# Storing eight bias rows once and repeating them from DRAM to DRAM, in place of eight stores that each repeat one partition's row

## The chip, the cores and the metric

The kernel runs on one core of a Trainium2 chip. A core has a matrix engine (PE, with its weight loads shown apart as PEld), a vector engine (DVE), a scalar engine (ACT), a general engine (POOL) and a sequencer that issues transfers (SP). Here all transfers are issued by SP, and 16 DMA engines carry them out. The metric is the time of one launch on the device in microseconds (us), lower is better. The median of three runs of the kernel before is 2368.28 us (2366.44 to 2369.18).

## The reference, cut to what matters

The program is two transformer blocks one after the other, on 1024 tokens of width 1024, in float32. The first block has a sparse attention branch (each query attends to 256 keys that an index score picks), a recurrent branch, a convolution branch, three gates and an MLP; the second block has latent attention and a pooling branch. The change touches the bias of the first block's attention. Each of the 8 heads adds a bias that depends only on the distance between query and key:

```
bias = rel_bias[_t5_bucket(t[None, :, None] - idx)]      # 32 buckets, 8 heads
logits = jnp.where(valid, logits + bias, -inf)
```

Beyond some distance the bucket is always the last one, so the bias is constant there; a constant added to all logits of a row drops out of the softmax. Only the near part, two blocks of 128 keys, has to be added, as a difference to that constant.

## The kernel before, in words

**The near bias.** Lines 667 to 681 make one row of 384 numbers for each head: a small matmul (line 672) of the bias table with a one-hot matrix gives an 8 x 384 result, from which DVE takes the far value away (line 676), into the tile `tr`: head h lies in partition h, 1536 bytes long. In the attention a tile of 128 queries by 256 keys needs this row shifted by one element for each query, that is, a different start in each partition. The kernel gets the shift from DRAM: the array `nbt` holds, for each head, the row of 384 numbers 128 times one after the other (192 KB for a head), and it is read back with a row length of 383 instead of 384 (line 681), so that each partition starts one element later. Lines 678 to 680 write `nbt`: eight transfers, one for each head, each of which reads the one partition of that head 128 times.

**Who reads it.** `unit_a` (line 730) is the first half of an attention unit for a pair of heads j and a block b of queries. At b = 7, the first block of each pair, it loads the near bias of the two heads from `nbt` into `nb_t`, a part of the constant tile `CP` (line 733, "CP<-nbt" in the trace); POOL adds it to the mask (line 743).

**What else SP issues there.** The weights come in pieces of 512 KB through `load_raw` (line 143; line 146 in the trace, "wr<-w_in", "wr<-w_up_conv") into two buffers `wr`. Each piece is split by `split_w` (line 194) into a high part H (ACT, which shows as line 138, "ws<-wr") and a rest L (POOL, line 199) in two buffers `ws`; a `wr` buffer is free again when POOL is done with it. PE multiplies from `ws` (`fm`, line 212, matmul at line 223): for each of the k tiles H times the high part of the data, H times its rest, and L times its high part. In the stretch where the near bias is written the program is in the loop of lines 625 to 633: a gate (a weight piece, 48 matmuls, a tanh on ACT, "th") and a mix with the convolution branch ("mx", stored by SP at line 632, "mix<-mx"), in turn. Between them run the steps of `search` (lines 495 to 588), which finds each query's 256th largest score bit by bit: DVE counts at line 535, ACT counts at line 538 ("jd<-sc,thrA"), and small DVE steps at lines 540 to 545.

**What sets the order.** The text of the kernel gives the data flow; the framework orders the instructions of each engine from it (the option `schedule_with_timeline_sim` in line 32) and adds the waits. Each engine, SP too, then runs its instructions in that fixed order: an instruction that waits holds up all that stand behind it on its engine. In the trace this order differs from the text: the rows of the near bias, which stand behind the loop of lines 625 to 633 in the text, are issued inside it, and the first two loads of `CP` from `nbt` stand between the fourth and the fifth of the eight stores.

Of the kernel before, what the change touches and what calls it, by code (L numbers as in the profile page):

```python
# [77 lines left out]
def tile_net(ctx: ExitStack, tc, a, out):  # L78
    nc = tc.nc
    PE, ACT, DVE, POOL, SP = nc.tensor, nc.scalar, nc.vector, nc.gpsimd, nc.sync  # L80
# [22 lines left out]
    def page(dt=F32, s="pg"):  # L103
        shape = [128, 4096 if dt == I8 else 2048 if dt == BF16 else 1024]
        if s in TEMPS:
            return tpp.tile(shape, dt, tag="tp", name=nm(s))
        return pgp.tile(shape, dt, tag="pg", name=nm(s))
# [12 lines left out]
    def stage(s="st", dt=F32):  # L120
        return stp.tile([128, 1024], dt, tag="st", name=nm(s))
# [7 lines left out]
    def dram(shape, s):  # L129
        return drp.tile(shape, F32, tag=s, name=s)  # L130
# [261 lines left out]
    for i in range(NB):  # L392
        j = page(s="junk")
# [13 lines left out]
    for j in range(2):  # L407
        for ps, cs in fm(next(wgen), hT):
            for e in range(2):
                S = SA[2 * j + e]  # L410
                o = 64 * e
# [263 lines left out]
    tr = stage("tr")  # L675
    DVE.tensor_scalar(out=tr[0:8, 0:384], in0=ps[0:8, 0:384], scalar1=far[0:8], scalar2=None, op0=ALU.subtract)
    nbt = dram([8, 128 * 384], "nbt")
    for h in range(8):
        SP.dma_start(out=nbt[h:h + 1].rearrange("o (p j) -> o p j", j=384),  # L679
                     in_=tr[h:h + 1, 0:384].unsqueeze(1).to_broadcast([1, 128, 384]))  # L680
        nbd.append(nbt[h, 127:127 + 383 * 128].rearrange("(p j) -> p j", j=383)[:, 0:256])

    VS, KK, QQ = [], {}, {}
# [839 lines left out]
    for pr_ in range(2):  # L1523
# [6 lines left out]
        for e in range(2):  # L1530
            o = 64 * e
# [203 lines left out]
```

## Time and profile before

| what | value |
| --- | --- |
| median of three runs | 2368.28 us (2366.44 to 2369.18) |
| the profiled execution's own time | 2365.88 us |
| its span, first to last instruction | 2364.0 us |
| PE busy | 2254.2 us, 95% of the span |
| DVE, ACT, POOL busy | 1442.4, 910.2 and 814.6 us |
| mean granted PE clock | 0.979 of full speed |
| all transfers | 228.89 MB on SP's queue, 31.8% of the 16 DMA engines' time |

The profile was taken of one execution; 1.88 us of its time lie outside its span. A busy share is an average over the whole span; what holds a stretch up is read from the waits and from the order of events inside that stretch. An issue on SP is short unless something keeps it: the time of an issue row is the time that SP spent on the instruction, not that of the transfer.

### The profile page before, as it was taken

To read this page: it belongs to the slowest core of one execution; us is meant where nothing else is said; L and a number is where in the kernel's file an instruction comes from. 1 tells how busy PE (TensorE), PEld (TensorE's weight loads), DVE (VectorE), ACT (ScalarE), POOL (GpSimd) and SP (SyncE) were. 2 spreads that over 40 slices of the span, in tenths; PEclk is the share of its full clock that TensorE was granted. 3 is DMA by queue.
4 is the path that set the end of the run, shared out by engine and by line. 5 is a ranking of instruction groups with operands and counts; after the bars stand their busy time and mean duration, and the time that the engine had idled before them with its cause. 6 is when DMAs were issued, how large, how long until landed. Compare 5 with 4: busy or idle time off the path is not lost.

```text
span 2364.0 us, 29829 instructions
## 1 busy us (share of the span) xinstructions
PE 2254.2 (95%) x11311; PEld 1899.9 (80%) x11311; DVE 1442.4 (61%) x2559; ACT 910.2 (39%) x1459; POOL 814.6 (34%) x524
## 2 busy tenths in 40 slices
PE   8999499999999999989999999998999999888998
PEld 6888387888888888878878888886888888677898
DVE  3589466354444377975576767595432768755655
ACT  5346241454445343523443333331111444345640
POOL 3221123344443222356245646322222236431036
PEclk9999799999999999999999999999999999899999
DMA  3113822212211211254233342652321254342341
GB/s 125 45 38 57 71 74 66 72 54 62 71 61 50 78 36 36 90 200 148 98 96 112 102 125 89 218 204 90 125 80 54 76 152 143 116 153 95 97 174 73
DMA packets 219076, 230.87 MB, mean 98 GB/s; under 512 B 12507, under 2 KB 189358, under 8 KB 218926
## 3 DMA queue, kind: packets, MB, share of 16 engines
q1 hardware_dynamic: 218926, 228.89, 31.8%
q8 instruction: 91, 1.49, 0.3%
q14 instruction: 59, 0.48, 0.1%
HBM read 166.47 MB, written 61.08 MB: 96 GB/s over the span
## 4 chain that ended last, share of the span: by engine, by line
PE 73%; DVE 12%; DMA 4%; issue 4%; POOL 3%; SPq 2%; ACT 2%; POOLq 0%; DVEq 0%; ACTq 0%
PE fm L223 43%; PE fm L354 15%; PE sp L1682 3%; PE sp L1566 2%; PE sp L262 1%; DVE jd L535 1%; PE sp L754 1%; PE py L790 1%; PE sp L910 1%; SPq L679 1%; PE sp L783 1%; DMA wr<-w_in 1%; DMA wr<-w_mlp_up 1%; POOL wf L329 1%; PE py L1608 1%
## 5 line engine op out<-in xcount | busy, mean ns | idle before, releaser
L223 PE MATMUL fm<-hH,ws 128*128 128x512 f32 (+1 forms) x1952 | 625.0, 395 | 32.3 <-ACT ws L138 31.8
L199 POOL TENSOR_TENSOR ws<-wr,ws 128x1024 fp32r<-128x1024 f32 (+2 forms) x123 | 288.7, 2347 | 851.9 <-ACT ws L138 805.6
L354 PE MATMUL fm<-xf,wf 128*128 128x512 f32 x2100 | 485.3, 392 | 1.6 <-POOL wf L329 0.9
L354 PEld LDWEIGHTS fm<-xf,wf 128*128 128x128 f32 x2100 | 395.6, 189 | 85.4 <-POOL wf L329 2.5
L223 PEld LDWEIGHTS fm<-hH,ws 128*128 128x128 f32 (+1 forms) x1952 | 366.2, 188 | 109.7 <-ACT ws L138 32.2
L223 PE MATMUL fm<-hL,ws 128*128 128x512 f32 (+1 forms) x976 | 386.1, 396 | 0.0
L223 PE MATMUL fm<-uH,ws 128*128 128x512 f32 x1024 | 319.6, 392 | 0.9 <-DVE x L1269 0.9
L138 ACT ACTIVATE ws<-wr 128x1024 fp32r<-128x1024 f32 (+2 forms) x124 | 126.0, 1016 | 417.4 <-PE fm L223 219.1
L223 PEld LDWEIGHTS fm<-uH,ws 128*128 128x128 f32 x1024 | 193.2, 189 | 41.9 <-DVE x L1269 1.1
L223 PEld LDWEIGHTS fm<-hL,ws 128*128 128x128 f32 (+1 forms) x976 | 184.0, 189 | 36.3
L329 POOL TENSOR_TENSOR wf<-sf,wf 128x512 fp32r<-128x512 f32 x100 | 152.8, 1537 | 150.5 <-ACT wf L138 141.7
L223 PE MATMUL fm<-uL,ws 128*128 128x512 f32 x512 | 199.9, 391 | 0.0
L362 DVE TENSOR_TENSOR kp<-kp,fm 128x512 f32<-128x512 f32 x167 | 113.9, 683 | 117.9 <-PE fm L354 111.6
L1269 DVE TENSOR_TENSOR x<-x,fm 128x512 f32<-128x512 f32 x128 | 87.0, 683 | 159.3 <-PE fm L223 152.8
L329 POOL TENSOR_TENSOR wf<-wr,wf 128x512 fp32r<-128x512 f32 x75 | 114.6, 1534 | 97.7 <-ACT wf L138 94.4
L138 ACT ACTIVATE p<-p,sml 128x896 f32<-128x896 f32 (+7 forms) x128 | 97.0, 773 | 65.1 <-DVE sml L760 41.3
L223 PE MATMUL fm<-spH,ws 128*128 128x512 f32 x352 | 116.5, 397 | 0.0
L223 PEld LDWEIGHTS fm<-uL,ws 128*128 128x128 f32 x512 | 96.6, 189 | 19.7
L189 DVE TENSOR_TENSOR PT<-sp,PT 128x512 fp32r<-128x512 f32 (+2 forms) x136 | 75.8, 576 | 59.6 <-ACT PT L138 58.4
L535 DVE TENSOR_SCALAR_CACHE_REDUCE jd<-sc,thrD 128x384 int8<-128x384 f32 (+1 forms) x124 | 100.6, 812 | 2.9
L138 ACT ACTIVATE jd<-sc,thrA 128x896 int8<-128x896 f32 (+1 forms) x62 | 67.8, 1094 | 48.2 <-DVE thrA L545 47.4
L138 ACT ACTIVATE PT<-sp 128x512 fp32r<-128x512 f32 (+2 forms) x136 | 64.7, 505 | 55.9 <-PE py L790 26.6
(395 smaller groups left out, 3882.5 us busy)
## 6 DMA issues: line engine op xcount, KB each, us to landing
wr<-w_in SPq DMA_DIRECT2D x78, 512.0 KB
wr<-w_mlp_up SPq DMA_DIRECT2D x32, 512.0 KB
ud<-t SPq DMA_DIRECT2D x32, 512.0 KB
wr<-w_mlp_down SPq DMA_DIRECT2D x32, 512.0 KB
uL<-ud SPq DMA_DIRECT2D x32, 512.0 KB
gate<-th SPq DMA_DIRECT2D x16, 512.0 KB
th<-gate SPq DMA_DIRECT2D x16, 512.0 KB
wr<-w_out SPq DMA_DIRECT2D x16, 512.0 KB
```

The costliest lines, as they stand in the source:

```text
L138: return ACT.activation(out=out, in_=in_, func=func, **kw)
L189: DVE.tensor_tensor(out=L, in0=src, in1=f(H), op=ALU.subtract)
L199: POOL.tensor_tensor(out=L, in0=v, in1=f(H), op=ALU.subtract)
L223: PE.matmul(ps[0:M], w_[:, k, :], x_[:, cs], start=(k == 0 and i == 0), stop=(k == kt - 1 and i == 2))
L262: PE.transpose(out=ps[:, (i - n0) * 128:(i - n0 + 1) * 128], in_=t, identity=ident[0:t.shape[0], 0:t.shape[0]])
L329: POOL.tensor_tensor(out=L, in0=src, in1=f(H), op=ALU.subtract)
L354: ins = PE.matmul(ps, w_[:, j, :], x_, start=(j == 0 and i == 0), stop=(j == J - 1 and i == 2))
L362: DVE.tensor_tensor(out=dst, in0=add, in1=ps, op=ALU.add)
L535: DVE.tensor_scalar(out=jd[:, 0:W], in0=sc[b][:, 0:W], scalar1=th[:, i:i + 1], scalar2=None, op0=ALU.is_ge, op1=ALU.add, accum_out=cnt[gna ...
L1269: DVE.tensor_tensor(out=x1[m][:, cs], in0=x1[m][:, cs], in1=ps, op=ALU.add)
L1566: PE.matmul(ps[:, 0:e - o], l_[:, qs], r_[:, cs], start=(n == 0), stop=(n == 4))
L1682: PE.matmul(po, l_[:, ts], r_, start=(k == 0 and n == 0), stop=(k == 7 and n == 2))
```

## The change

The eight stores of the loop become two transfers. The first stores the 8 x 384 tile once, one row from each partition, into a new DRAM array `nbr` (12 KB). The second, which depends on the first, reads each of the eight rows of `nbr` 128 times and writes all of `nbt` (1.5 MB). What `nbt` holds, its readers and all else stay.

```
     nbt = dram([8, 128 * 384], "nbt")
+    nbr = dram([8, 384], "nbr")
+    SP.dma_start(out=nbr, in_=tr[0:8, 0:384])
+    SP.dma_start(out=nbt.rearrange("h (p j) -> h p j", j=384), in_=nbr.unsqueeze(1).to_broadcast([8, 128, 384]))
     for h in range(8):
-        SP.dma_start(out=nbt[h:h + 1].rearrange("o (p j) -> o p j", j=384),
-                     in_=tr[h:h + 1, 0:384].unsqueeze(1).to_broadcast([1, 128, 384]))
         nbd.append(nbt[h, 127:127 + 383 * 128].rearrange("(p j) -> p j", j=383)[:, 0:256])
```

## Rows read from the trace of the kernel before

**Rows 1.** The page, part 2: the span in 40 equal slices of 59.1 us.
```profile
PE   8999499999999999989999999998999999888998
...
PEclk9999799999999999999999999999999999899999
```

**Rows 2.** Waits, 220 to 292 us: total us, times, longest us.
```profile
ACT ws L138 <- DMA wr<-w_in: 34.0, 1, 34.0
...
PE fm L223 <- ACT ws L138: 31.8, 1, 31.8
```

**Rows 3.** Timeline of PE, 252 to 292 us: start us, us, what.
```profile
251.75 0.39 PE L223 MATMUL fm<-spL,ws 128*128 128x512 f32 x1
...
254.01 0.39 PE L223 MATMUL fm<-spH,ws 128*128 128x512 f32 x1
286.23 0.79 PE L223 MATMUL fm<-hH,ws 128*128 128x512 f32 x1 [31.82 <-ACT ws L138]
...
290.75 0.40 PE L223 MATMUL fm<-hL,ws 128*128 128x512 f32 x1
```

**Rows 4.** Timeline of SP, 180 to 300 us: start us, us, issues.
```profile
187.01 0.37 SPq L146 DMA_DIRECT2D wr<-w_up_conv  x1
...
224.80 13.12 SPq L679 DMA_DIRECT2D nbt<-tr  x4
237.96 14.39 SPq L733 DMA_DIRECT2D CP<-nbt  x2
252.40 13.62 SPq L679 DMA_DIRECT2D nbt<-tr  x4
266.13 7.11 SPq L146 DMA_DIRECT2D wr<-w_in  x1
...
280.73 0.38 SPq L146 DMA_DIRECT2D wr<-w_in  x1
```

**Rows 5.** Stretches: us, busy of each engine, granted clock, DMA share, GB/s.
```profile
225.00:226.00 1.00, 1.00 (x6) 0.84 (x5) 0.96 (x3) 1.00 (x2) 0.00 (x0) 1.00 0.98 385
...
240.00:244.00 4.00, 4.00 (x19) 3.34 (x18) 3.93 (x7) 1.54 (x3) 2.38 (x1) 1.00 0.84 26
...
260.00:266.00 6.00, 0.00 (x0) 0.00 (x0) 0.00 (x0) 0.00 (x0) 0.00 (x0) 0.50 0.87 27
...
283.00:284.00 1.00, 0.00 (x0) 0.00 (x0) 0.00 (x0) 0.00 (x0) 0.00 (x0) 0.50 1.10 361
```

**Rows 6.** Chain that ended last, 215 to 345 us: start us, us, what.
```profile
224.24 0.53 DVE tr L676
...
266.13 18.90 DMA wr<-w_in
```

**Rows 7.** Timeline of POOL, 185 to 330 us.
```profile
235.34 2.40 POOL L199 TENSOR_TENSOR ws<-wr,ws 128x1024 fp32r<-128x1024 f32 x1 [13.14 <-ACT ws L138]
...
286.25 2.37 POOL L199 TENSOR_TENSOR ws<-wr,ws 128x1024 fp32r<-128x1024 f32 x1 [42.24 <-ACT ws L138]
```

**Rows 8.** Timeline of ACT, 232 to 292 us.
```profile
250.59 0.58 ACT L138 ACTIVATE th<-fm 128x512 f32<-128x512 f32 x1
285.12 1.06 ACT L138 ACTIVATE ws<-wr 128x1024 fp32r<-128x1024 f32 x1 [33.95 <-DMA wr<-w_in]
```

**Rows 9.** Stretches around one weight load (columns as in rows 5).
```profile
188.00:189.00 1.00, 1.00 (x6) 0.84 (x5) 0.96 (x3) 0.97 (x3) 0.00 (x0) 1.00 0.81 170
189.00:190.00 1.00, 1.00 (x6) 0.81 (x5) 1.00 (x3) 0.83 (x2) 0.00 (x0) 1.00 1.00 352
190.00:191.00 1.00, 1.00 (x6) 0.84 (x5) 1.00 (x2) 0.00 (x0) 0.00 (x0) 1.00 0.01 2
```

**Rows 10.** Stretch while `ln_g_2` (line 1644) is read 128 times (columns as rows 5).
```profile
2244.00:2244.50 0.50, 0.50 (x6) 0.50 (x6) 0.50 (x1) 0.50 (x2) 0.00 (x0) 1.00 0.90 352
```

**Rows 11.** Stretch behind the stall (columns as in rows 5).
```profile
340.00:350.00 10.00, 10.00 (x46) 8.28 (x45) 0.00 (x0) 1.84 (x3) 1.41 (x1) 1.00 0.32 100
```

**Rows 12.** Waits on transfers elsewhere, whole span: total us, times, longest us.
```profile
ACT wf L138 <- DMA wr<-w_mlp_up: 57.2, 8, 9.0
```

## The prediction, made before the changed kernel was run

> **What bounds the kernel now.** I read the page's slices first. PE is busy in nine tenths of nearly every slice; the one that stands out is the fifth (236 to 295 us), with PE at 4 tenths and a granted clock of 7 tenths [rows 1]. The waits of that stretch say why: PE waits 31.8 us, once, for the split of a weight piece on ACT, and ACT waits 34.0 us, once, for a transfer of `w_in` [rows 2]. PE's own timeline puts the hole between 254.0 and 286.2 us [rows 3]. All engines stand still in it [rows 5], since each has work in its fixed order that needs PE or ACT.
>
> The timeline of SP shows what kept the transfer [rows 4]. The eight stores of `nbt` begin at 224.80, as soon as DVE has written `tr` [rows 6]. The eight stores and the two loads of `CP` among them take SP 41 us to issue (13.12 + 14.39 + 13.62): the queue behind them is full, so each issue waits for room. The `w_in` piece that PE will miss is issued only at 266.13 and is used by ACT 18.9 us later [rows 4, 6]. Its buffer had been free since 237.74, when POOL ended the split before last (235.34 + 2.40) [rows 7]. So SP's order and its full queue delay it, nothing else.
>
> Why the queue is full is in the stretches: while the stores run, the DMA engines are busy 0.84 to 0.87 of the time and move only 26 to 27 GB/s [rows 5]. Around it, storing a full 128-partition tile goes at 385 GB/s and loading a weight piece at 361 [rows 5]. Eight stores of 196,608 bytes at 27 GB/s are 58 us. What sets them apart is their source, one partition read 128 times.
>
> **The change part by part.**
>
> *Removed: eight stores, 58 us of transfer and about 27 us of SP.* The gain is not these 58 us but what PE loses by them. PE's first matmul behind the hole begins at 286.23; without it, it would follow the one at 254.01 by the usual step. That step is 0.226 us: between 251.75 and 254.01 ten matmuls begin one after the other [rows 3]. So it would begin at 254.24: 31.99 us earlier. [...] That is 2.49 us more [rows 3]. Together 34.5 us.
>
> *Added: one store of 12 KB and a wait.* SP issues it at 224.8, waits until it has landed, and issues the repeat. An unqueued weight load shows such a round trip: issued at 187.01, moving in 188 to 190, nothing left after 190 [rows 4, 9]; 3.0 us in all, of which 512 KB (524,288 bytes) at 361 GB/s take 1.45, so some 1.6 us are fixed. I give the small store the whole 3.0, since a tile's store stands ahead of it. The repeat is issued at 227.8. Nothing behind SP's wait is due: the next weight buffer is free at 237.74 only [rows 7]. Cost nothing.
>
> *Added: the repeat, 1,572,864 bytes from DRAM to DRAM.* No row shows a transfer with both ends in DRAM. From one side, each end alone: 361 to 385 GB/s [rows 5], and reading one DRAM row 128 times is no hindrance by itself (`ln_g_2` for 128 partitions: 352 GB/s) [rows 10]. That gives 4.4 us. From the other side, the 27 GB/s of the stores if the destination were to blame: 58 us. I take 8.7 us, half the load's rate, because both ends load the same memory; it is nearest to the rows with a DRAM end. With 1.6 us fixed it lands at 227.8 + 1.6 + 8.7 = 238.1.
>
> *Moved: the wait of the `CP` loads.* Before, each needed its head's store; now both need the whole repeat, and SP stands still until then if they keep their place ahead of the `w_in` piece. Behind them are that piece and the mix store. Two issues of 0.4 us put the piece at 238.9; the CP loads' 262 KB take 0.7 us of its way, so it lands at 238.9 + 0.7 + 3.0 = 242.6.
>
> When is it due? Not before 251.2: ACT's order has the tanh of 250.59 (0.58 us) ahead of that split [rows 8]. So 8.6 us are to spare, and the repeat may take up to 17.3 us (91 GB/s) before anyone waits for it. From there each further us costs one. ACT's split then ends at 252.2 and POOL's, 2.4 us [rows 7], at 254.7; PE can begin at 254.24 with the two matmuls that need H alone and wants L at 254.69. What is left of the hole is 0.1 us, or 0.2 to be careful.
>
> *What is late next.* DVE's and ACT's work in the hole's place moves with PE. Behind it DVE has room: it stands idle from 340 to 350 while PE is full [rows 11], so PE sets the pace and carries the gain on. All later work waits for work, not for a time of day; I find nothing that gives it back.
>
> [...] The trace shows all sixteen engines at work on the old stores, 0.84 to 0.87 busy [rows 5]. [...]
>
> The sum: 34.5 - 0.2 = 34.3 us. The profiled execution took 2365.88 us (a span of 2364.0 and 1.88 outside), so it would take 2331.6. It was 2.4 us under the median of 2368.28; on the median the forecast is 2334.0.
>
> **The rivals.**
>
> *The repeat is slow, and part of the hole stays.* For it: no row shows such a transfer, and few engines or one memory at both ends could bring it below 91 GB/s. Against it: every row with a DRAM end is at over three times that. At 60 GB/s it takes 26 us, 9 past the limit; the half clock comes back too (2.5), so the gain is 34.3 - 11.5 = 22.8: 2345.5. At 42 GB/s (37 us) it is 2356.5.
>
> *Slower: the destination is what is slow, and the `CP` loads wait for all of it.* Before, SP went on behind the stores of two heads; now it stands until all eight are written. With 58 us the repeat lands at 227.8 + 1.6 + 58 = 287.4, the piece at 287.4 + 0.8 + 0.7 + 3.0 = 291.9, and ACT begins its split 6.8 us later than at 285.12 [rows 8]: 2375. It decides from 51 us on (31 GB/s). Were the repeat to run on a single engine, a sixteenth of 361 GB/s, it would take 70 us: 2387. Against it: the mix store writes DRAM at 385 GB/s [rows 5].
>
> *The order changes elsewhere.* The framework orders the whole program from its own reckoning, in which eight transfers become two. SP's order already differs from the text [rows 4], so a piece may now come sooner or later somewhere. The nearest price is what late weight pieces cost elsewhere: eight waits of 57.2 us in all on ACT, 9.0 the longest [rows 12]. I take two average ones of 7.2, 15 us, to either side of the forecast: 2319 to 2349. For it speaks only that nothing fixes the order; against it, that the changed transfers hang together with nothing but the `CP` loads, whose reader comes only in the attention, behind the whole search.
>
> **How the numbers follow.** The forecast, hole gone and order as before: 0.60. A slow repeat: 0.15. Slower: 0.08. Another order: 0.17. The likeliest gives 2334. The range goes from 2322 to 2356: it leaves out the slower case (0.08), a repeat beyond 37 us (some 0.03) and the ends of another order (some 0.04). About 0.2% (4.7 us) is what a measurement of this kernel can tell from no change. Faster by more than that: 0.60, 0.13 of the slow repeat and 0.15 of the other orders, 0.88; within it 0.04; slower 0.08.
>
> **What would show it.** Right, if PE's hole between 254 and 286 is gone, the fifth slice has PE and clock at 9, SP issues the `w_in` piece by 247 in place of 266.13, ACT's wait of 34.0 us for it is gone, and DVE still has its idle stretch before the end of the search. The repeat's duration shows as the stretch of high DMA share behind 228 us: 8.7 us by my value. Wrong, if that stretch is longer than 17 us and ACT still waits for the piece; or if the hole is gone and PE's idle time turns up elsewhere, in another order of its work. If DMA engines stay busy at 27 GB/s, the partition was not to blame and the main step falls.

## The result, and the profile after

The changed kernel takes 2332.26 us (median of 4 runs, 2330.53 to 2334.7) against 2368.28 (2366.44 to 2369.18): a ratio of 0.985, 95% interval 0.9833 to 0.9867. The forecast was 2334.0, in 2322 to 2356, with 0.88 on faster. The profiled execution took 2330.53 us, its span is 2328.3 us.

The page of the changed kernel, part 2 (40 slices of 58.2 us), against [rows 1]: the fifth slice is as full as the others, with the clock at full (1.00 in the stretches from 220 to 290 us).

```profile
PE   8999999999999999899999999989999999889998
...
PEclk9999999999999999999999999999999999899999
```

PE's timeline there, against [rows 3] (start us, us, what): the matmul that came 31.99 us late now follows the last one of the mix by one usual step.

```profile
253.74 0.39 PE L223 MATMUL fm<-spH,ws 128*128 128x512 f32 x1
253.97 0.39 PE L223 MATMUL fm<-hH,ws 128*128 128x512 f32 x1
254.20 0.39 PE L223 MATMUL fm<-hL,ws 128*128 128x512 f32 x1
```

SP's timeline, against [rows 4]. Two issues stand in place of eight, none of these issues takes longer than 0.81 us, and the `w_in` piece goes out at 238.29 in place of 266.13.

```profile
224.54 0.29 SPq L679 DMA_DIRECT2D nbr<-tr  x1
226.86 0.80 SPq L680 DMA_DIRECT2D nbt<-nbr  x1
237.37 0.81 SPq L734 DMA_DIRECT2D CP<-nbt  x2
238.29 0.38 SPq L146 DMA_DIRECT2D wr<-w_in  x1
```

SP's own waits, 200 to 292 us (total us, times, longest): the two that the change brought.

```profile
SPq L734 <- DMA nbt<-nbr: 9.7, 1, 9.7
...
SPq L680 <- DMA nbr<-tr: 2.0, 1, 2.0
```

Stretches of the changed kernel (columns as in [rows 5]; the last two are DMA share and GB/s): the repeat moves from 228.4 to 237.0 us, at 194 to 206 GB/s in the full microseconds between, half of the engines busy (share 0.52 to 0.54). DVE still has its idle stretch before the end of the search, from 300 to 316 us here.

```profile
228.00:229.00 1.00, 1.00 (x6) 0.84 (x5) 0.96 (x9) 0.40 (x2) 0.00 (x0) 1.00 0.30 88
...
230.00:231.00 1.00, 1.00 (x6) 0.84 (x5) 0.96 (x3) 1.00 (x2) 0.00 (x0) 1.00 0.53 198
...
300.00:316.00 16.00, 16.00 (x72) 13.28 (x71) 3.66 (x8) 3.21 (x4) 4.79 (x3) 1.00 0.32 99
```

ACT and POOL split the piece when their order reaches it, against [rows 7, 8]; neither waits for a transfer. POOL's first row is the split that frees the buffer for the piece.

```profile
250.81 1.05 ACT L138 ACTIVATE ws<-wr 128x1024 fp32r<-128x1024 f32 x1
```

```profile
235.10 2.40 POOL L199 TENSOR_TENSOR ws<-wr,ws 128x1024 fp32r<-128x1024 f32 x1 [13.15 <-ACT ws L138]
...
251.94 2.40 POOL L199 TENSOR_TENSOR ws<-wr,ws 128x1024 fp32r<-128x1024 f32 x1 [8.17 <-ACT ws L138]
```

PE's 11311 matmuls stand in the same order in both traces, so the same matmul can be compared by its place. The 1080th begins 0.27 us earlier in the changed kernel, the 1120th 34.75 us, the last 36.24. The hole and the slow clock behind it are 34.75 - 0.27 = 34.48 us of that. The other 1.8 us come before 224 us (0.27) and, mostly, near 650 us, far from any changed instruction; in two kernels below with the same median time, e1 and e3, the lead over the kernel before is 0.14 and 1.04 us at the 1080th, 34.62 and 35.52 at the 1120th, which is 34.48 in both again, and 33.0 and 35.2 at the end. I take what lies outside the hole for the spread between executions.

### The profile page after: what moved, and what is told of

Same layout as the page of the kernel before. It is cut to its first block, busy times and chain, and to the rows that moved or that the text cites. A ratio compares the mean times of both kernels' runs of the same rounds, so it can differ in the third digit from the quotient of the medians.

```text
span 2328.3 us, 29820 instructions
## 1 busy us (share of the span) xinstructions
PE 2249.2 (97%) x11311; PEld 1896.3 (81%) x11311; DVE 1441.3 (62%) x2559; ACT 910.1 (39%) x1459; POOL 813.2 (35%) x524
## 4 chain that ended last, share of the span: by engine, by line
PE 81%; DVE 9%; issue 3%; POOL 2%; DMA 2%; ACT 2%; SPq 0%; DVEq 0%; POOLq 0%; ACTq 0%
PE fm L223 49%; PE fm L354 16%; PE sp L1683 3%; PE sp L1567 2%; PE sp L262 1%; PE sp L755 1%; PE py L791 1%; PE sp L911 1%; PE sp L784 1%; DMA wr<-w_mlp_up 1%; PE py L1609 1%; POOL wf L329 1%; DVE mt L1136 0%; DVE PT L189 0%; DVE bc L271 0%
## 5 line engine op out<-in xcount | busy, mean ns | idle before, releaser
L329 POOL TENSOR_TENSOR wf<-sf,wf 128x512 fp32r<-128x512 f32 x100 | 152.7, 1536 | 151.8 <-ACT wf L138 141.6
L189 DVE TENSOR_TENSOR PT<-sp,PT 128x512 fp32r<-128x512 f32 (+2 forms) x136 | 75.8, 576 | 59.2 <-ACT PT L138 58.2
```

The source lines that it names most:

```text
L189: DVE.tensor_tensor(out=L, in0=src, in1=f(H), op=ALU.subtract)
L329: POOL.tensor_tensor(out=L, in0=src, in1=f(H), op=ALU.subtract)
```

## The experiments

Theory: sixteen engines that all read one SBUF partition move 27 GB/s; the queue behind these stores delays one weight piece past the moment when PE needs it; the piece has some 8 us to spare, and each us beyond costs one. The rivals are the number of transfers, the writing of DRAM, and SP's waits. "Above" is the median less 2332.3. The kernel before, run again beside each set of these, had medians of 2367.0 to 2367.4 us, about 1 us under the 2368.28 above; the ratios go by these.

| run | edit | median us (range) | ratio to before [95%] | above |
| --- | --- | --- | --- | --- |
| e1 | eight repeats, from DRAM | 2332.02 (2330.86 to 2333.32) | 0.9848 [0.9831, 0.9864] | -0.3 |
| e6 | one transfer, one partition | 2372.24 (2370.74 to 2374.28) | 1.0019 [1.0008, 1.0029] | 39.9 |
| e2 | one transfer, eight partitions | 2344.74 (2343.92 to 2346.59) | 0.9904 [0.9887, 0.992] | 12.4 |
| e9 | partitions 0 and 1 | 2379.47 (2375.55 to 2380.6) | 1.0049 [1.0026, 1.0072] | 47.2 |
| e10 | partitions 0 and 4 | 2347.72 (2343.71 to 2350.86) | 0.9917 [0.9888, 0.9946] | 15.4 |
| e3 | copies outermost | 2332.3 (2330.93 to 2335.12) | 0.9855 [0.9838, 0.9871] | 0.0 |
| e4 | chain of two repeats | 2338.02 (2335.07 to 2341.4) | 0.9874 [0.9858, 0.9891] | 5.7 |
| e7 | chain of three repeats | 2347.4 (2345.64 to 2351.34) | 0.9913 [0.9896, 0.9929] | 15.1 |
| e5 | four repeats, no wait | 2346.41 (2344.14 to 2348.48) | 0.991 [0.9893, 0.9926] | 14.1 |
| e8 | old stores, spread out | 2333.92 (2330.68 to 2335.02) | 0.9854 [0.9837, 0.987] | 1.6 |

### The source or the number: e1 and e6

e1 keeps the row store and makes eight transfers of the repeat again:

```
-    SP.dma_start(out=nbt.rearrange("h (p j) -> h p j", j=384), in_=nbr.unsqueeze(1).to_broadcast([8, 128, 384]))
+    for h in range(8):
+        SP.dma_start(out=nbt[h:h + 1].rearrange("o (p j) -> o p j", j=384),
+                     in_=nbr[h:h + 1].unsqueeze(1).to_broadcast([1, 128, 384]))
```

> The row store to DRAM stays, but the repeat is again eight transfers, one for each head, now read from DRAM. Theory (the source, one SBUF partition read by all engines at once, was slow): the eight repeats run at 350 to 390 GB/s on sixteen engines, 0.5 us each, 4.2 us in all; PE has no hole between 254 and 286, time 2332 +- 3 as for the changed kernel. Rival (eight transfers fill SP's queue, their number is what costs): SP still stalls for some 7 us an issue, the w_in piece goes out after 260, the hole stays: 2360 to 2370.

e6 is one transfer again, without the row store, all of it from partition 0:

```
-    SP.dma_start(out=nbr, in_=tr[0:8, 0:384])
-    SP.dma_start(out=nbt.rearrange("h (p j) -> h p j", j=384), in_=nbr.unsqueeze(1).to_broadcast([8, 128, 384]))
+    SP.dma_start(out=nbt.rearrange("h (p j) -> (h p) j", j=384).unsqueeze(0),
+                 in_=tr[0:1, 0:384].unsqueeze(1).to_broadcast([1, 1024, 384]))
```

> One transfer, whose 1024 reads all go to the first head's partition; so all heads get head 0's bias row, the other seven rows are left out. Theory (the one partition is slow, not the number of transfers): 27 GB/s, 58 us, SP waits for all of it before the CP loads, the w_in piece lands near 289 against 285 before, hole some 3 us longer than before: 2368 to 2374. Rival (number of issues): one issue instead of eight, no hole, 2332.

SP's timeline of e1: eight transfers with the `CP` loads among them, as before, but none is held for 7 us, and the piece goes out at 237.67. One of its stretches is behind it.

```profile
227.02 1.88 SPq L681 DMA_DIRECT2D nbt<-nbr  x3
230.67 0.35 SPq L736 DMA_DIRECT2D CP<-nbt  x1
231.06 0.47 SPq L681 DMA_DIRECT2D nbt<-nbr  x1
231.63 0.53 SPq L736 DMA_DIRECT2D CP<-nbt  x1
232.21 2.39 SPq L681 DMA_DIRECT2D nbt<-nbr  x4
237.67 0.39 SPq L146 DMA_DIRECT2D wr<-w_in  x1
```

```profile
232.00:233.00 1.00, 1.00 (x6) 0.83 (x5) 0.98 (x7) 0.41 (x1) 0.00 (x0) 1.00 0.79 238
```

SP's timeline of e6, and a stretch of it: one issue of 0.61 us, then 59 us until the `CP` loads may go, at the old 27 GB/s.

```profile
223.83 0.61 SPq L679 DMA_DIRECT2D nbt<-tr  x1
283.88 0.83 SPq L734 DMA_DIRECT2D CP<-nbt  x2
284.81 0.38 SPq L146 DMA_DIRECT2D wr<-w_in  x1
```

```profile
260.00:264.00 4.00, 0.00 (x0) 0.00 (x0) 0.00 (x0) 0.00 (x0) 0.00 (x0) 0.50 0.87 27
```

e1's time and its missing hole came as expected, its rate did not: from 229 to 236 us, the `CP` loads among them, the stretches of 1 us show 72 to 299 GB/s and not 350 to 390, and why was not tried.

The number of transfers and the writing of DRAM are out; the source is what counts. e6 is also the prediction's slower rival made real: one transfer in place of eight, SP standing until all of it has landed, and the time 0.2% above before (interval 0.1 to 0.3%).

### What a partition shares: e2, e9, e10

e2 has `in_=tr[0:8, 0:384].unsqueeze(1).to_broadcast([8, 128, 384])`, the eight partitions in one transfer with no copy in DRAM. In e9 and e10 two engines read one partition each:

```
+    SP.dma_start(out=nbt.rearrange("h (p j) -> (h p) j", j=384).rearrange("(t p) j -> t p j", t=2),
+                 in_=tr[0:2, 0:384].unsqueeze(1).to_broadcast([2, 512, 384]))        # e9; e10: tr[0:8:4, 0:384]
```

> No DRAM copy of the rows: one transfer reads the eight partitions of the tile, each 128 times, and writes all of the repeated array. Theory A (sixteen engines on one partition is what is slow, each partition has its own limit): eight engines read one partition each at about 65 ns a packet, 8 us in all as from DRAM, time 2332 +- 3, and the wait for the row store (2.0 us on SP) is gone. Theory B (neighbouring partitions share one limit): all eight together run at 27 to 54 GB/s, 29 to 58 us; at 54 the piece comes some 9 us late (2343 to 2346), at 27 the hole is as long as before or longer, 2368 to 2375.

> One transfer, the same bytes, from partitions 0 and 1 only, each read 512 times by one engine of its own (two engines); the heads get only the rows of heads 0 and 1. It asks why eight partitions together gave 52 GB/s. Theory N (neighbouring partitions share one limit of some 27 GB/s): 27 GB/s, about 110 ns a packet, 58 us, hole as before or longer, 2366 to 2374. Theory P (each partition has its own limit): each engine runs at its own pace of 65 ns a packet, 47 GB/s, 33 us, 2345 to 2350. Theory E (an engine that reads one partition needs 215 ns a packet, as with eight): 14 GB/s, 110 us, above 2410.

> The same with partitions 0 and 4 in place of 0 and 1, two engines again; the heads get the rows of heads 0 and 4. Theory N (the limit is shared by partitions 0 to 3 and another by 4 to 7, which makes two times 27 GB/s for the eight): the two do not share, 65 ns a packet, 47 GB/s, 33 us, 2345 to 2350. If the limit is shared by all eight partitions: 27 GB/s, 2366 to 2374. Theory P: 2345 to 2350 as well. Theory E: above 2410.

A stretch of each, e2, e9 and e10 in this order (last two columns DMA share and GB/s):

```profile
240.00:244.00 4.00, 4.00 (x20) 3.30 (x19) 3.93 (x10) 1.10 (x2) 2.39 (x1) 1.00 0.45 51
```

```profile
240.00:250.00 10.00, 10.00 (x46) 8.29 (x45) 9.72 (x28) 6.10 (x11) 2.39 (x1) 1.00 0.12 25
```

```profile
240.00:250.00 10.00, 10.00 (x46) 8.28 (x45) 9.72 (x27) 6.10 (x11) 2.40 (x1) 1.00 0.13 50
```

In e9 and e10 two of sixteen engines are busy (0.12 and 0.13), and partitions 0 and 4 give twice what 0 and 1 give (50 against 25 GB/s). Eight partitions in a row give no more than those two: 51 (e2). So the limit is not each partition's own: 0 and 1 share one, 0 and 4 do not. That is theory B of e2, at 54 GB/s, and, for the two pairs that ran, N of the two others; which more of the eight share was not tried. The packets of 1536 bytes say the same: the median one took 785 ns on its engine before the change and in e6, 215 in e2, 119 in e9, and 65 in e10 and in the changed kernel. Only e9's time lies outside its range, 5.5 us above: from its issue to the `CP` loads 63.4 us pass (224.81 to 288.18), 3.3 more than e6's 60.1. Why two engines on two neighbours are slower than sixteen on one partition was not tried.

### Eight engines or sixteen: e3

```
+    SP.dma_start(out=nbt.rearrange("h (p j) -> p h j", j=384), in_=nbr.unsqueeze(0).to_broadcast([128, 8, 384]))
```

> The same single repeat from DRAM with the 128 copies as the outermost dimension in place of the 8 heads. If eight engines set the repeat's pace (share 0.53, about 200 GB/s, 8.2 us in the changed kernel), sixteen take it: share 1.0 or above, 370 to 400 GB/s, 4.2 us, and the CP loads are issued 4 us sooner. If memory at both ends sets it, share rises to 1.0 at the same 200 GB/s and it still takes 8 us. The time is 2332 +- 3 by both, since the piece behind it is not due before 251.

Stretches of e3, where the same bytes are repeated with 128 as the outermost dimension:

```profile
229.00:230.00 1.00, 1.00 (x6) 0.84 (x5) 0.96 (x4) 0.97 (x2) 0.00 (x0) 1.00 1.06 310
...
231.00:232.00 1.00, 1.00 (x6) 0.84 (x5) 0.96 (x8) 0.29 (x1) 0.00 (x0) 1.00 1.03 190
```

The share doubles from 0.53 to above 1.0, with 128 in place of 8 outermost. The rate does not: it is 190 to 316 GB/s, and issue to `CP` load shrinks by 2.0 us (226.24 to 234.73, 8.5 against 10.5), not by the 4 that I expected. Neither reading held alone. In the changed kernel the eight engines set the pace: a packet takes 65 ns on its engine, as in e10, whose source is not DRAM and where only two engines are at work. In e3 the median is 65 as well but the mean is 96 (67 in the changed kernel), so something holds the sixteen up at times; e3 also writes the rows in another order (eight rows 192 KB apart, then the next eight), and the two were not tried apart. The time stays, as both said.

### How much the piece has to spare: e4, e7, e5

e4 and e7 put one or two repeats ahead, each read from the one before; in e5 three repeats without a wait go into arrays that nobody reads; SP issues them behind the one that is read.

```
+    for i in range(1):                       # e4; 2 in e7
+        nbx = dram([8, 128 * 384], f"nbx{i}")
+        SP.dma_start(out=nbx.rearrange("h (p j) -> h p j", j=384), in_=nbr.unsqueeze(1).to_broadcast([8, 128, 384]))
+        nbr = nbx[:, 127 * 384:128 * 384]    # e5: three times, without this line
```

> The repeat twice, one after the other: the rows are repeated into an array that nobody else reads, and the array that is read is repeated from that one's last row of each head, so SP waits for two landings. Each link took 10.5 us in the changed kernel (226.86 to 237.37). Theory (8 to 9 us to spare before the piece is due at 250.8, each further us costs one): the second lands at 247.9, the piece goes out at 248.3 and lands near 252, PE loses 1 to 2.5 us: 2332 to 2336. Rival (SP's wait costs from the first us on): 10 us more than the changed kernel, 2342.

> Three repeats in a chain, each from the one before. The piece's transfer stands behind the third repeat in SP's order but does not wait for its landing; SP issues it at 248.8, and eight of the engines are busy with the third repeat until about 257. Theory: the piece lands near 260, ACT's split begins 9 us late, PE loses 9 us and perhaps 2.5 more at half clock: 2340 to 2345. Rival (the hole of the kernel before had another cause than transfers ahead of the piece): no hole, 2332.

> Four repeats from the same rows with no waits between them, three of them into arrays that nobody reads, queued behind the one that is read. SP is not held by a landing but eight engines' queues hold 33 us of work. Theory (what delays the piece is the transfers ahead of it in the engines' queues): the last repeat ends near 261.5, the piece lands near 264, PE loses 13 us and 2.5 at half clock: 2345 to 2349. Rival (only SP's waits matter, the engines take the piece beside the repeats): the piece lands before 251, 2332.

SP's timelines of e4, of e7 and of e5. In the chains SP waits for landings; in e5 the queue is full, as before the change [rows 4]: three issues take 17.87 us.

```profile
226.55 0.80 SPq L682 DMA_DIRECT2D nbx<-nbr  x1
236.84 0.65 SPq L684 DMA_DIRECT2D nbt<-nbx  x1
249.44 0.34 SPq L738 DMA_DIRECT2D CP<-nbt  x1
249.88 0.39 SPq L146 DMA_DIRECT2D wr<-w_in  x1
```

```profile
249.39 0.63 SPq L684 DMA_DIRECT2D nbt<-nbx  x1
250.12 2.50 SPq L146 DMA_DIRECT2D wr<-w_in  x1
```

```profile
226.80 17.87 SPq L682 DMA_DIRECT2D nbx<-nbr  x3
244.77 8.49 SPq L737 DMA_DIRECT2D CP<-nbt  x2
253.37 0.40 SPq L146 DMA_DIRECT2D wr<-w_in  x1
```

ACT's waits for the piece in e4, e7 and e5, in this order:

```profile
ACT ws L138 <- DMA wr<-w_in: 3.4, 1, 3.4
```

```profile
ACT ws L138 <- DMA wr<-w_in: 13.9, 1, 13.9
```

```profile
ACT ws L138 <- DMA wr<-w_in: 12.8, 1, 12.8
```

These waits are of one execution, and the medians scatter by some us, so I compare within each trace: how much less the lead over the kernel before grows from the 1080th to the 1120th matmul than the 34.48 us of the changed kernel. PE loses 5.9, 15.5 and 13.1 us there in e4, e7 and e5, with 3.4, 13.9 and 12.8 us of waiting on ACT; before the change it is 34.5 with 34.0. The other runs fit: 13.5 with 12.4 (e2), 14.9 with 13.1 (e10), 39.7 with 39.1 (e6), 43.4 with 42.7 (e9), and 0.0 in e1, e3 and e8, where ACT does not wait for a transfer. So time follows the lateness of this one piece, whether the queue or a landing makes it late, one for one and 0.3 to 2.5 us on top. e5 fell in its range. e7 came out 2.4 us above its range and e4 2.0 above, partly because the second link of a chain took 12.6 us (236.84 to 249.44) where the first took 10.3; it reads rows that lie 192 KB apart, and why that is slower was not tried. The rest of e4 is the clock. PE stood still twice, 1.26 and 1.25 us, and its timeline shows what followed:

```profile
253.41 0.39 PE L223 MATMUL fm<-spH,ws 128*128 128x512 f32 x1
255.06 0.50 PE L223 MATMUL fm<-hH,ws 128*128 128x512 f32 x1 [1.26 <-ACT ws L138]
...
255.87 0.39 PE L223 MATMUL fm<-hL,ws 128*128 128x512 f32 x1
257.51 1.22 PE L223 MATMUL fm<-hH,ws 128*128 128x512 f32 x2 [1.25 <-POOL ws L199]
...
263.62 0.39 PE L223 MATMUL fm<-hL,ws 128*128 128x512 f32 x1
```

```profile
258.00:260.00 2.00, 2.00 (x6) 1.52 (x6) 1.93 (x7) 1.52 (x3) 0.00 (x0) 0.50 0.69 188
...
264.00:266.00 2.00, 2.00 (x11) 1.61 (x10) 1.66 (x6) 0.33 (x1) 0.00 (x0) 1.00 0.00 0
```

Fourteen matmuls begin from 257.51 to just before 263.62, 6.11 us where 14 steps of 0.226 are 3.16. The granted clock is 0.50 in 258 to 262 and 1.00 from 264. The two stops cost 2.8 us of PE (the steps at 255.06 and 257.51 are 1.42 and 1.41 us too long), the clock behind them 3.0 more: together 5.8 of the 5.9 in this trace. The median is 5.7 above, the profiled execution itself 7.2.

### The burst or the bytes: e8

The kernel before, its eight stores kept, but one in each round of the gate and mix loop (the building of `tr` stands ahead of the loop):

```
         SP.dma_start(out=mixd[m], in_=mx)
+        q = 32 * (1 + m % 3)
+        trm = CP[q:q + 8, 344:728]
+        DVE.scalar_tensor_tensor(out=trm, in0=mx[0:8, 0:384], scalar=0.0, in1=tr, op0=ALU.mult, op1=ALU.add)
+        SP.dma_start(out=nbt[m:m + 1].rearrange("o (p j) -> o p j", j=384),
+                     in_=trm[m:m + 1, 0:384].unsqueeze(1).to_broadcast([1, 128, 384]))
```

> The eight old stores, each 128 reads of one partition, kept in number, source and bytes, but one in each round of the gate and mix loop: a small DVE step in each round copies the rows behind that round's mix, and the store of one head goes from the copy. Eight DVE steps of about 0.5 us are added. Theory (a store of 7.2 us fits in the 8 to 12 us that a piece has to spare, only the burst of eight does not): no hole of 30 us, 2332 to 2340. Rival (58 us of slow transfers cost PE 32 us wherever they stand): eight small holes, 2360 to 2370.

SP's timeline of e8, one of its stretches and two waits from 300 to 375 us: a store every 16 us, the engines busy 0.9 of the time, and PE full. The stores are as slow as before: their packets' median is 800 ns.

```profile
237.90 0.50 SPq L647 DMA_DIRECT2D nbt<-CP  x1
238.50 0.54 SPq L146 DMA_DIRECT2D wr<-w_in  x1
...
254.13 0.49 SPq L647 DMA_DIRECT2D nbt<-CP  x1
```

```profile
240.00:248.00 8.00, 8.00 (x37) 6.62 (x36) 7.75 (x26) 5.25 (x9) 2.40 (x1) 1.00 0.90 108
```

```profile
PE sp L672 <- ACT sq L138: 4.5, 1, 4.5
DVE cs L580 <- DMA mix<-mx: 2.4, 1, 2.4
```

The same 58 us of slow transfers cost next to nothing when no piece has to stand behind more than one of them: 2333.92 us, and its interval overlaps with the changed kernel's. In its trace nothing is lost at the hole's place. Behind the eighth store SP waits 8.4 us for its landing before it issues a `CP` load, the last mix store stands behind that (issued at 344.52), DVE waits 2.4 us for it, and PE then stands 4.5 us where it stands 2.8 in the changed kernel (line 656 there). These 1.7 us are about what e8 is above; one execution shows them. So the loss was the burst ahead of a due piece, not the slow bytes as such. No version among these is measurably faster than the changed kernel.

## Why the prediction was right, point by point

- *The hole and the clock behind it, 34.5 us.* Measured by the same matmul's place: 34.48. The medians differ by 36.0; the rest lies outside the hole and was not forecast. The split of the 34.5 is a little off. The 2.49 us put to the clock are what the nine matmuls behind the hole took over nine usual steps (4.52 against 2.03 [rows 3], at a granted clock of 0.50 from 286 to 290); some 0.6 of them are a second wait, PE's for the rest L from POOL, at 288.68 in the trace before (a step of 1.01 us where the one ahead of it is 0.43).

```profile
288.68 1.22 PE L223 MATMUL fm<-hH,ws 128*128 128x512 f32 x2 [0.38 <-POOL ws L199]
```

- *The row store, 3.0 us to landing, cost nothing.* SP waited 2.0 us for it, and the repeat went out 2.3 us after the store was issued. Nothing was due.
- *The repeat, 8.7 us, landing at 238.1.* It moved for 8.6 us and let the `CP` loads go at 237.37. The value came from halving the load's rate because both ends are DRAM. That reason was not the right one: eight engines did it (share 0.53; sixteen engines show 1.03 to 1.14 in e3, so 0.53 is about half), each at the same 65 ns a packet as e10's two, and sixteen engines went beyond 200 GB/s (e3). That the wrong reason gave the right value is luck. The 361 GB/s behind it was also misread: in that microsecond a weight piece and the mix store move together. Alone a piece moved at 352 [rows 9], which makes 8.9 in place of 8.7.
- *The `CP` loads' wait.* 9.7 us of SP, ending 0.1 us before the piece could have gone at the earliest (237.37 against 235.10 + 2.40 = 237.50); the piece went at 238.29, forecast 238.9.
- *8.6 us to spare, then one for one.* e4, e7 and e5 show the slope. The threshold is only bracketed: the piece is in time when it goes out at 238.29 and makes ACT wait 3.4 us at 249.88 (e4); with a slope of one the last harmless moment is 246.5, 8.2 us behind the first, and no run lies between. Two terms were left out: in e4 the clock cost as much again as two short stops (3.0 against 2.8 us), and a chain's later link is slower (12.6 against 10.3 us in e4).
- *Residual of 0.2 us.* None is seen; PE goes on after the usual step.
- *The rival "slower".* Its premise, a slow destination, is refuted by e1, which writes the same array at 72 to 299 GB/s; its mechanism, SP standing for the whole repeat, is shown by e6 (59 us).
- *The rival "the repeat is slow".* e2 and e10 come near it by other means: their transfers take some 31 us but go out earlier, so that the `CP` loads go at 256.94 and 257.63, where the rival's 26 us would let them go at 255.4 (227.8 + 1.6 + 26). They took 2344.74 and 2347.72; the prediction has 2345.5 for it. The argument against it, that every row with a DRAM end is at over three times 91 GB/s, overlooks the old stores themselves, which end in DRAM at 27.
- *The rival "another order".* All engines but SP kept their order; SP's differs only in the changed transfers.
- *What blocked the source.* The prediction said "one partition read 128 times". e9 and e10 mend this: two neighbouring partitions, 0 and 1, are no better than one (25 against 27 GB/s), and 0 and 4 together are twice as fast (50).

## What to carry to other kernels

Look for transfers that keep all DMA engines busy at a fraction of the usual rate (here 0.87 busy at 27 GB/s, where a weight piece alone moved at 352), and ask which weight or tile stands behind them in the queue: the price is that piece's lateness, not the transfer's length. A broadcast out of one SBUF partition is such a transfer, and one out of the neighbours 0 and 1 was no faster (25); read it from DRAM (194 to 206 GB/s), or spread it between the loads (e8, 2333.92 us). Before a faster path is tuned further, work out the slack of what waits behind it: here 8.6 us of transfer (the changed kernel) and 6.7 (e3) gave the same time, and by the prediction's estimate anything under some 17 us would have.

## What the runs showed of the hardware that I had not expected

- Two engines reading SBUF partitions 0 and 1 move 25 GB/s, reading 0 and 4 they move 50; eight partitions 0 to 7 with eight engines (share 0.44 to 0.48) move 51 to 55, one partition with sixteen engines 27.
- From DRAM to DRAM, 1.57 MB in pieces of 1536 bytes move at some 200 GB/s on eight engines and at 190 to 316 on sixteen, which also wrote in another order.
- Two stops of PE of 1.26 and 1.25 us, 2.5 us apart, were followed by half clock (0.50 granted from 258 to 262): fourteen matmuls took 6.1 us in place of 3.2, as much loss as the 2.8 us of the stops.
